# A hybrid attention trunk on one core: earlier loads for a triangular solve, loads in program order, and copies moved between engines

## Chip, core and metric

The kernel runs on one core of a Trainium2 chip. The metric is device time in microseconds (us): three runs of the kernel before took 3787.65, 3792.02 and 3792.04 us, median 3792.02.

The core has five engines, each with its own queue of instructions, worked off strictly in order: TensorE (PE in the profile; PEld is its loading of stationary operands), VectorE (DVE), ScalarE (ACT), GpSimd (POOL) and SyncE (SP), which here issues nearly all transfers (DMAs). SPq is SyncE's queue of DMA issues. Engines wait for each other by semaphores.

## What is computed

The reference is one layer of a transformer-like trunk over 2048 latent tokens (16 tiles of 128) and 256 context tokens (2 tiles), model width 1024:

```python
def sandwich_block(x, mod, g_norm, mixer, w_gu, w_down):
    sh1, sc1, gt1, sh2, sc2, gt2 = mod
    h = rmsnorm(x, g_norm[0]) * (1.0 + sc1) + sh1
    m, extra = mixer(h)
    x = x + gt1 * rmsnorm(m, g_norm[1])
    h = rmsnorm(x, g_norm[2]) * (1.0 + sc2) + sh2
    gate, up = jnp.split(h @ w_gu, 2, axis=-1)
    f = (jax.nn.silu(gate) * up) @ w_down
    x = x + gt2 * rmsnorm(f, g_norm[3])
    return x, extra
```

The mixer projects h by one matrix `w_in` and feeds three groups of heads: A is softmax attention with normalised and rotated queries and keys, B is a gated DeltaNet in both directions with a short convolution (its chunks of 64 need the inverse of a unit lower triangular matrix, `triangular_solve`), C is neighbourhood attention. Their outputs are joined and multiplied by `w_out`.

## The kernel before

The stages follow each other on TensorE, all in fp32 that is split into a high and a low part (`hi`, `lo`), so that each product takes three matmuls (`mm3`).

- **Phase B** (`phase_b`, to about 308 us): the adaLN vectors, h for six blocks of three tiles (stored to DRAM as `h_d`), the projection for group B, and its convolution. `conv(b)` runs one block late; for the last block the taps are added as each projection ends, and `conv_out` takes SiLU of it (L340), transposes it on TensorE and copies it out on VectorE (L353) to `y_d` (L354).
- **Phase AC** (`phase_ac`, to about 824 us) has two sweeps over the 18 tiles of h. The first multiplies each tile by three slices of 384 columns of `w_in` (c_cols: q, k, v of group C), the second by two of 320 columns (a_cols: q, k, v of group A) and, for the last three tiles, the third slice left over. One unit is one tile by one slice: 24 matmuls. A slice of weights comes in four pieces (`load_w`: tile wraw, three buffers) that ACT rounds (L255) and DVE subtracts (L256). Tiles of h (hi, lo, three buffers each) are loaded by `h_next`, one ahead per finished tile. In the second sweep each unit's result is copied by ACT (zn, four buffers, L449), normalised by head (L451 to L458, with POOL's power at L91), rotated on DVE and POOL (L470 to L475) and stored (zo).
- **Background work** rides on these sweeps. `Background.run(us)` takes pieces of a generator, each with an estimated cost, as long as its credit lasts. `prep` makes the DeltaNet operands of all tiles (it begins with `gates`). `bg` is the solve: five batches of up to 128 systems, three for the recurrence's first half. Each batch loads its systems from DRAM (B at L828, A at L829, tiles sB and sA), builds a matrix in sW (L833), and works through 76 pairs of a product (L843, into stmp) and a sum (L844) on DVE, each needing the one before; it ends with a copy (L847, into the same buffer as sA) and stores (L850, L851). sA and sW have one buffer, so a batch's loads wait for the stores of the batch before. A batch costs 26.9 of credit by the code's estimates. The third batch must be finished before group A begins (`need_solves(0)`), then `k_dups(4)` makes the last keys (KA, L1022 and L1023).
- **Group A** (to about 1625 us) runs one more piece of the solve per unit of 128 queries (L1242), **group C** follows (to about 1980 us), then the **output stage** (`phase_out`, to about 2225 us). There the weights `w_out` are scaled and split once (L1638 ACT, L1639 DVE) and each tile is multiplied, normalised and transposed; `h2_store` scales the transposed tile on ACT on its way out of PSUM (L1672, eight copies of 128 by 128 per tile). The **FFN** takes the rest.

The order on each queue is made when the program is built. The framework gives each instruction a priority by its place in the program, simulates the engines with its own cost estimates, and whenever an engine is free lets it take the ready instruction of highest priority. `tc.high_priority(offset=n)` moves instructions up by n places. `InOrder` (L28) pins an instruction behind everything traced before it on its engine, as long as its `on` is set; `self.sp` and `self.pe` are such wrappers, plain `nc.sync` is not. A pool's memory is by default waited for as a whole when a new pool takes its place; with `reuse_waits="tile"` each new tile waits only for the old tiles under it.

The lines around which the change turns are these:

```python
            for n in range(3):
                with tc.high_priority(offset=2 * HP if n == 0 else 0):
                    w = self.load_w(1680 + 384 * n, 384, wp, f"s{n}", ww=384, q=nc.scalar if n < self.WQ else None)
                Wc.append((c_cols, n, w, range(NT if n < 2 else NT - HB)))
                h_next()
            self.sp.dma_start(cos, a["cos"])
```

## Time and profile before

| | |
|---|---|
| median of three runs | 3792.02 us (3787.65 to 3792.04) |
| the profiled execution | 3788.4 us |
| its span, first to last instruction | 3786.6 us, mean granted clock 0.981 |
| PE busy in the span | 3608.3 us (95%) |
| DVE, ACT, POOL busy | 63%, 45%, 16% |
| DMA | 501.14 MB, mean 132 GB/s |

A row of the stretches gives a stretch in us from the span's start, its length, then busy us and count of instructions for PE, PEld, DVE, ACT and POOL, the share of full clock that was granted to TensorE, the busy share of the DMA engines and GB/s. A row of waits reads: engine, tile and line that waited, what it waited for, us in total, times, longest. A row of a timeline has start, duration, engine, line, operation, tiles and count. L37 is the wrapper through which TensorE's and much of SyncE's work is issued, so there the tile tells what it is. Durations come from one profiled execution; ends of matmuls are modelled.

### The profile page before, as it was taken

The page shows a single profiled execution, that of the slowest core. Times are in us where ns is not written, and L with a number is a line of the kernel's source. Part 1 is how long each engine was busy: PE and PEld are TensorE (multiplying, and loading weights), DVE is VectorE, ACT ScalarE, POOL GpSimd, SP SyncE. Part 2 cuts the span into 40 slices and gives each one's busy share as a digit, 9 for nine tenths or more (in the row PEclk, how much of TensorE's full clock was granted, in tenths as well). Part 3 has the DMA queues.
Part 4 walks back from the last instruction along what each step waited for, and adds up shares of the span by engine and source line. Part 5 has one row for each costly group of instructions (what it writes and reads, how often), then busy time and mean ns, then how long its engine had stood idle before and what let it go on. Part 6 is the DMA issues. An engine that isn't in the chain of part 4 may idle for free.

```text
span 3786.6 us, 64734 instructions
## 1 busy us (share of the span) xinstructions
PE 3608.3 (95%) x24526; PEld 3161.6 (83%) x24526; DVE 2399.1 (63%) x5030; ACT 1719.6 (45%) x3533; POOL 587.8 (16%) x859
## 2 busy tenths in 40 slices
PE   8997999979999999989999989999999999999999
PEld 5887988966777777768887879999999999888887
DVE  4784477689755555558775667778778777422433
ACT  4223222226666666656775653334334333322321
POOL 0002321630000000000003411111111111000121
PEclk9998999989999999999999999999999999999999
DMA  7555877842111221155315653334334332634653
GB/s 267 205 205 181 255 223 220 210 116 53 48 51 53 53 53 51 48 138 164 100 51 174 214 174 100 100 98 126 98 102 123 98 102 87 199 110 129 202 181 128
DMA packets 647496, 501.14 MB, mean 132 GB/s; under 512 B 253505, under 2 KB 576944, under 8 KB 644624
## 3 DMA queue, kind: packets, MB, share of 16 engines
q1 hardware_dynamic: 644400, 493.40, 43.3%
q8 instruction: 193, 3.16, 0.4%
q10 hardware_dynamic: 2624, 3.55, 0.3%
q14 instruction: 119, 0.97, 0.1%
q0 software_dynamic: 160, 0.05, 0.0%
HBM read 348.14 MB, written 148.73 MB: 131 GB/s over the span
## 4 chain that ended last, share of the span: by engine, by line
PE 74%; DVE 13%; ACT 4%; POOL 3%; DMA 3%; issue 3%; SPq 0%; ACTq 0%; POOLq 0%; DVEq 0%
PE pd L37 15%; PE Y L37 10%; PE pso L37 9%; PE pt L37 7%; PE X L37 7%; PE Z L37 6%; PE po L37 6%; PE rx L37 3%; PE m L37 2%; PE Sa L37 2%; DVE stmp L843 2%; PE S L37 2%; PE Sb L37 2%; DVE mx L1220 2%; DVE sW L844 1%
## 5 line engine op out<-in xcount | busy, mean ns | idle before, releaser
L1034 ACT ACTIVATE PT<-pt 128x512 f32<-128x512 f32 (+1 forms) x600 | 332.3, 554 | 257.9 <-PE pt L37 251.2
L37 PE MATMUL Y<-hop,raw 128*128 128x384 f32 x1788 | 338.6, 338 | 7.0 <-DVE u L1877 3.7
L37 PEld LDWEIGHTS Y<-hop,raw 128*128 128x128 f32 x1788 | 315.5, 188 | 8.6 <-DVE u L1877 4.7
L37 PE MATMUL po<-PT,V 128*64 128x256 f32 (+1 forms) x3072 | 314.8, 342 | 2.2 <-ACT PT L1034 1.9
L37 PE MATMUL pso<-whi,hi 128*128 128x384 f32 (+2 forms) x864 | 289.1, 335 | 24.8 <-ACT whi L255 13.0
L37 PE MATMUL pt<-ident,P 128*128 128x128 f32 x1752 | 285.1, 280 | 15.5 <-ACT PT L1034 7.9
L37 PE MATMUL pso<-whi,lo 128*128 128x384 f32 (+2 forms) x864 | 282.9, 327 | 8.4 <-DMA lo<-hl 8.4
L37 PE MATMUL pso<-wlo,hi 128*128 128x384 f32 (+2 forms) x864 | 283.1, 328 | 0.7 <-DVE wlo L256 0.5
L37 PEld LDWEIGHTS pt<-ident,P 128*128 128x128 f32 x1752 | 200.3, 141 | 94.8 <-ACT PT L1034 35.8
L37 PEld LDWEIGHTS po<-PT,V 128*64 128x64 f32 x3072 | 181.5, 137 | 79.2 <-issue 33.8
L37 PE MATMUL X<-hop,raw 128*128 128x384 f32 x1176 | 224.8, 339 | 3.4 <-DVE raw L1742 3.4
L37 PE MATMUL Z<-hop,raw 128*128 128x384 f32 x1188 | 223.6, 336 | 0.0
L1742 DVE TENSOR_TENSOR raw<-S,raw 128x512 fp32r<-128x512 f32 x198 | 145.9, 738 | 113.1 <-ACT raw L1741 108.1
L37 PEld LDWEIGHTS X<-hop,raw 128*128 128x128 f32 x1176 | 209.4, 189 | 4.1 <-DVE raw L1742 4.1
L37 PEld LDWEIGHTS Z<-hop,raw 128*128 128x128 f32 x1188 | 208.7, 187 | 0.1
L1889 POOL TENSOR_TENSOR o<-sg,p 128x384 f32<-128x384 f32 x66 | 89.2, 1351 | 740.7 <-DVE p L1888 365.8
L1741 ACT ACTIVATE raw<-S 128x512 fp32r<-128x512 f32 x198 | 124.6, 630 | 174.6 <-PE X L37 66.6
L37 PEld LDWEIGHTS pso<-whi,hi 128*128 128x128 f32 x864 | 168.5, 195 | 29.4 <-ACT whi L255 14.5
L37 PE MATMUL pd<-wd,ao 128*128 128x512 f32 x756 | 185.5, 394 | 0.0
L37 PE MATMUL pd<-wd,hop 128*128 128x512 f32 x756 | 183.0, 392 | 0.0
L971 POOL TENSOR_TENSOR rSe<-rS,eh 64x128 f32<-64x128 f32 x144 | 54.9, 400 | 810.6 <-DVE rS L1003 779.9
L37 PEld LDWEIGHTS pso<-whi,lo 128*128 128x128 f32 x864 | 168.0, 194 | 11.7 <-DMA lo<-hl 10.1
(346 smaller groups left out, 8273.9 us busy)
## 6 DMA issues: line engine op xcount, KB each, us to landing
hr<-a SPq DMA_DIRECT2D x72, 704.0 KB, 4.5
wr<-in_w_gu_dram SPq DMA_DIRECT2D x66, 512.0 KB, 4.0
wr<-in_w_gu_dram SPq DMA_DIRECT2D x132, 256.0 KB, 3.1
a<-o SPq DMA_DIRECT2D x396, 64.0 KB, 1.6
wm<-in_w_mod_dram SPq DMA_DIRECT2D x48, 512.0 KB, 4.2
hi<-hh SPq DMA_DIRECT2D x36, 512.0 KB, 5.2
lo<-hl SPq DMA_DIRECT2D x36, 512.0 KB, 6.0
st<-ptk SPq DMA_DIRECT2D x18, 768.0 KB, 4.2
```

Source lines behind the costliest of these rows:

```text
L37: r = f(*x, **kw)
L843: v.tensor_tensor(tv, M[:n, c0:c1, c0:i], M[:n, c0:i, i].unsqueeze(1).to_broadcast([n, m, k]), ALU.mult)
L844: v.tensor_reduce(M[:n, c0:c1, i], tv, AX.X, ALU.add)
L971: nc.gpsimd.tensor_tensor(Se[hh[x], d], S[hh[x], d, :, hh[x]], e.unsqueeze(2).to_broadcast([64, 2, 64]), ALU.mult)
L1034: self.nc.scalar.activation(out, p, AF.Copy)
L1220: nc.vector.tensor_reduce(mx[:, i:i + 1], S[:, :hi_ - lo_], AX.X, ALU.max)
L1741: self.nc.scalar.activation(hi, raw, AF.Copy)
L1742: self.nc.vector.tensor_tensor(lo, raw, hi.bitcast(F32), ALU.subtract)
L1889: nc.gpsimd.tensor_tensor(o[:, 0], sg, p1, ALU.mult)
```

## The change

- The loads of `dt_bias` and `a_log` move from `gates` (in phase AC) to the second block of phase B, into tiles of their own. Those of cos, sin and the norm gains gq move from the start of the first sweep to after its tiles 8 and 10.
- At the start of the first sweep the loads of h and of weights are pinned in program order: h of tile 0, first weights, h of tiles 1 and 2, second and third weights. Pools hp2 and wp2 take the finer reuse waits.
- The last block's `conv_out` gets priority over everything around it.
- The solve: the loads of each batch's systems get top priority. In the second sweep its pieces are taken only up to tile 11, 1.15 instead of 0.8 of credit a unit, and at raised priority. In group A it is 1.1 instead of 2.0 a unit. By the code's credits the third batch then ends at tile 8 of the second sweep (before: tile 12), the fourth at unit 17 of group A (7), the fifth at unit 41 (21).
- The output weights are split by halves of 512 columns, one tile for each half.
- `h2_store` makes four of its eight copies per tile on DVE.
- A one-column tile of the output stage shares another's buffers (s2, rss).

```diff
@@ -61,7 +61,7 @@
     INAC, ST = False, False
-    SW, SA = (4.2, 1.8, 3.4), 0.8
+    SW, SA = (4.2, 1.8, 3.4), 1.15
@@ -305,6 +305,7 @@
             nc.sync.dma_start(self.mi, a["mi"])
+            self.dt, self.al = self.ctile("dt", [128, 8]), self.ctile("al", [128, 8])
@@ -385,9 +386,13 @@
                     conv(b - 1)
+                if b == 1:
+                    nc.sync.dma_start(self.dt, a["dt_bias"].rearrange("o d h -> o (d h)").to_broadcast([128, 8]))
+                    nc.sync.dma_start(self.al, a["a_log"].rearrange("o d h -> o (d h)").to_broadcast([128, 8]))
                     self.mod_part(1 if b == 1 else 2, sb, xp, psm)
-            conv_out(NB - 1, yl)
+            with tc.high_priority(offset=3000):
+                conv_out(NB - 1, yl)
@@ -402,8 +407,8 @@
             cst = es.enter_context(tc.tile_pool(name="pin_c", bufs=1))
-            hp = es.enter_context(tc.tile_pool(name="hp2", bufs=HB))
-            wp = es.enter_context(tc.tile_pool(name="wp2", bufs=1))
+            hp = es.enter_context(tc.tile_pool(name="hp2", bufs=HB, reuse_waits="tile"))
+            wp = es.enter_context(tc.tile_pool(name="wp2", bufs=1, reuse_waits="tile"))
@@ -547,7 +552,11 @@
                                 prep.run(us)
-                                self.bg.run(us2 if prep.left else us3)
+                                if w == 0:
+                                    self.bg.run(us2 if prep.left else us3)
+                                elif t0 < 12:
+                                    with tc.high_priority(offset=HP):
+                                        self.bg.run(us3)
@@ -555,18 +564,29 @@
             Wc = []
+            self.sp.on = True
             for n in range(3):
+                if n < 2:
+                    h_next()
                 with tc.high_priority(offset=2 * HP if n == 0 else 0):
-                    w = self.load_w(1680 + 384 * n, 384, wp, f"s{n}", ww=384, q=nc.scalar if n < self.WQ else None)
+                    w = self.load_w(1680 + 384 * n, 384, wp, f"s{n}", ww=384)
                 Wc.append((c_cols, n, w, range(NT if n < 2 else NT - HB)))
-                h_next()
-            self.sp.dma_start(cos, a["cos"])
-            self.sp.dma_start(sin, a["sin"])
-            gsrc = a["g_qk_a"]
-            self.sp.dma_start(gq[:, 0:6, :], gsrc[0, 0:1, :].unsqueeze(1).to_broadcast([128, 6, 64]))
-            self.sp.dma_start(gq[:, 6:8, :], gsrc[0, 1:2, :].unsqueeze(1).to_broadcast([128, 2, 64]))
-            nc.vector.tensor_scalar(gq[:, 0:6, :], gq[:, 0:6, :], 0.125, None, ALU.mult)
-            sweep(0, Wc, *self.SW)
+                if n == 0:
+                    h_next()
+            self.sp.on = self.INAC
+
+            def rotary(t):
+
+                if t == 8:
+                    self.sp.dma_start(cos, a["cos"])
+                    self.sp.dma_start(sin, a["sin"])
+                if t == 10:
+                    gsrc = a["g_qk_a"]
+                    self.sp.dma_start(gq[:, 0:6, :], gsrc[0, 0:1, :].unsqueeze(1).to_broadcast([128, 6, 64]))
+                    self.sp.dma_start(gq[:, 6:8, :], gsrc[0, 1:2, :].unsqueeze(1).to_broadcast([128, 2, 64]))
+                    nc.vector.tensor_scalar(gq[:, 0:6, :], gq[:, 0:6, :], 0.125, None, ALU.mult)
+
+            sweep(0, Wc, *self.SW, rotary)
@@ -650,10 +670,7 @@
         nc.scalar.activation(self.beta, self.ba[:, :, 0:8], AF.Sigmoid)
-        dt = wk.tile([128, 8], F32, name="dt")
-        al = wk.tile([128, 8], F32, name="al")
-        self.sp.dma_start(dt, a["dt_bias"].rearrange("o d h -> o (d h)").to_broadcast([128, 8]))
-        self.sp.dma_start(al, a["a_log"].rearrange("o d h -> o (d h)").to_broadcast([128, 8]))
+        dt, al = self.dt, self.al
@@ -825,8 +842,9 @@
                 r0 = 128 * e + 64 * bi if bi < 2 else 16 * e
-                nc.sync.dma_start(B[q], self.bt_d[bi // 2][r0:r0 + ns, fs])
-                nc.sync.dma_start(A[q], self.low_d[e][bi].rearrange("s (j i) -> s j i", j=64)[:, fs, fs])
+                with self.tc.high_priority(offset=3000):
+                    nc.sync.dma_start(B[q], self.bt_d[bi // 2][r0:r0 + ns, fs])
+                    nc.sync.dma_start(A[q], self.low_d[e][bi].rearrange("s (j i) -> s j i", j=64)[:, fs, fs])
@@ -1239,7 +1257,7 @@
                             nc.vector.reciprocal(rs[:, qi, h2:h2 + 1], sm[:, 3:4] if n > 1 else sm[:, 0:1])
-                            self.bg.run(2.0)
+                            self.bg.run(1.1)
@@ -1600,7 +1618,7 @@
                 self.mm3(mt[t][:, s], [hi[:, k] for k in range(KD)], [lo[:, k] for k in range(KD)],
-                         [WH[k][:, s] for k in range(KD)], [WL[k][:, s] for k in range(KD)])
+                         [WH[n][:, k] for k in range(KD)], [WL[n][:, k] for k in range(KD)])
@@ -1611,7 +1629,7 @@
                 sq = wk.tile([128, 1024], BF16, tag="rjunk", name="sq2", bufs=1)
-                s2 = wk.tile([128, 1], F32, tag="s2", name="s2")
+                s2 = wk.tile([128, 1], F32, tag="rss", name="s2")
@@ -1627,16 +1645,18 @@
             v.tensor_copy(ym[:, 5:8], self.goc)
-            WH, WL = [], []
+            WH, WL = [[cst.tile([128, KD, 512], F32R, name=f"W{x}{n}") for x in "HL"] for n in range(2)]
+            WH, WL = [WH[0], WL[0]], [WH[1], WL[1]]
                 raw = self.wraw[k]
-                WH.append(cst.tile([128, 1024], F32R, name=f"WH{k}"))
-                WL.append(cst.tile([128, 1024], F32R, name=f"WL{k}"))
-                nc.scalar.activation(WH[k], raw, AF.Copy, scale=ym[:, k:k + 1])
-                v.scalar_tensor_tensor(WL[k], raw, ym[:, k:k + 1], WH[k].bitcast(F32), ALU.mult, ALU.subtract)
+                for n in range(2):
+                    r = raw[:, 512 * n:512 * n + 512]
+                    nc.scalar.activation(WH[n][:, k], r, AF.Copy, scale=ym[:, k:k + 1])
+                    v.scalar_tensor_tensor(WL[n][:, k], r, ym[:, k:k + 1], WH[n][:, k].bitcast(F32), ALU.mult,
+                                           ALU.subtract)
@@ -1669,8 +1689,12 @@
                 k = 4 * g + j
-                self.nc.scalar.activation(h2[:, k], p[:, 128 * j:128 * j + 128], AF.Identity,
-                                          bias=self.b2[:, vv, k:k + 1], scale=self.s2[:, vv, k:k + 1])
+                if g:
+                    self.nc.vector.tensor_scalar(h2[:, k], p[:, 128 * j:128 * j + 128], self.s2[:, vv, k:k + 1],
+                                                 self.b2[:, vv, k:k + 1], ALU.mult, ALU.add)
+                else:
+                    self.nc.scalar.activation(h2[:, k], p[:, 128 * j:128 * j + 128], AF.Identity,
+                                              bias=self.b2[:, vv, k:k + 1], scale=self.s2[:, vv, k:k + 1])
```

## Prediction

> **What bounds the kernel now.** The first part of the page was read first, then busy time by stretch, then the waits of TensorE in the worst stretches, then the queue that issues DMAs (SPq) behind those waits.
>
> ```profile
> span 3786.6 us, 64734 instructions
> PE 3608.3 (95%) x24526; PEld 3161.6 (83%) x24526; DVE 2399.1 (63%) x5030; ACT 1719.6 (45%) x3533; POOL 587.8 (16%) x859
> ```
>
> TensorE is busy for 95% of the span, and the change takes no matmul away. So it can win only from the 178 us in which PE stands idle, and from the time in which it runs at half clock. The stretches say where that is (columns: stretch, length, busy time and count of PE, PEld, DVE, ACT, POOL, granted clock, DMA share, GB/s).
>
> ```profile
> 307.00:365.00 58.00, 35.99 (x157) 30.42 (x156) 21.64 (x52) 18.16 (x36) 13.25 (x42) 0.71 0.75 233
> 500.00:600.00 100.00, 87.87 (x557) 79.74 (x556) 78.21 (x225) 25.62 (x47) 31.71 (x33) 0.93 0.72 218
> 650.00:660.00 10.00, 7.86 (x41) 7.20 (x41) 9.64 (x32) 3.51 (x12) 0.32 (x2) 0.83 0.42 121
> 662.00:742.00 80.00, 73.95 (x497) 72.67 (x496) 47.62 (x130) 20.47 (x57) 55.72 (x104) 0.99 0.81 208
> 752.00:822.00 70.00, 51.62 (x313) 50.12 (x311) 58.65 (x218) 11.89 (x32) 29.02 (x49) 0.90 0.38 101
> 822.00:850.00 28.00, 18.23 (x80) 13.63 (x80) 20.68 (x66) 13.67 (x28) 3.50 (x12) 0.76 0.67 162
> 850.00:1000.00 150.00, 142.47 (x1302) 105.52 (x1300) 136.00 (x440) 102.44 (x215) 8.00 (x20) 1.00 0.24 60
> 1000.00:1150.00 150.00, 148.24 (x1454) 113.35 (x1454) 83.60 (x181) 103.34 (x212) 9.09 (x24) 1.00 0.18 50
> 2220.00:2260.00 40.00, 25.16 (x133) 23.39 (x132) 28.99 (x35) 25.98 (x49) 2.55 (x5) 0.87 0.67 207
> ```
>
> Three places matter: the seam into the first sweep (307 to 365, 22.0 us idle), the end of the second sweep with the start of group A (752 to 850, 28.2 us idle), and the seam into the FFN (2220 to 2260, 14.8 us idle). The half clock costs besides: at 0.71 over 58 us, 16.8 us of clock are missing, so PE was granted half speed for 33.6 us; the long waits below lie in 16.6 us of that, and the other 17 us of half-speed work lose 8.5 us. Hence the first seam costs 30.5 us.
>
> **Seam into the first sweep: small loads moved, loads in program order, last convolution first.** TensorE's waits between 300 and 365 (us in total, times, longest), then the queue SPq by time (start, us), and one row of the chain that ended last:
>
> ```profile
> PE pso L37 <- ACT whi L255: 13.0, 2, 11.5
> PE pso L37 <- DMA lo<-hl: 5.1, 1, 5.1
> PE pst L37 <- DVE es L353: 3.1, 2, 1.8
> ```
>
> ```profile
> 324.74 1.03 SPq L354 DMA_DIRECT2D y<-es  x1
> ...
> 338.09 0.65 SPq L37 DMA_DIRECT2D gq<-in_g_qk_a_dram  x1
> ...
> 339.81 8.00 SPq L37 DMA_DIRECT2D al<-in_a_log_dram  x1
> 347.86 1.91 SPq L37 DMA_DIRECT2D wraw<-in_w_in_dram  x2
> ```
>
> ```profile
> 314.64 7.97 DMA lo<-hl
> ```
>
> The 11.5 us wait is for the second weight slice. Its last two wraw pieces are issued at 347.86, right behind the load of a_log, which held the queue for 8.00 us behind the many small rows of gq. After the change dt and al are loaded in phase B, cos and sin at tile 8 and gq at tile 10 of the sweep. The queue may stand for the same 8.00 us there; three tiles of h are held then, three units of 24 matmuls each per tile, so I cost that at nothing. If that cover were gone it would cost those 8 us again.
>
> The new order on SPq is h of tile 0, first weights, h of tiles 1 and 2, second and third weights, pinned behind everything traced earlier on that queue: the last store of y. That store (now at 324.7 and later) needs the last SiLU on ACT; beside it two rows of the DMA issues, whose last column is the median time to landing:
>
> ```profile
> 301.71 2.13 ACT L340 ACTIVATE yl<-yl 128x2304 f32<-128x2304 f32 x1 [2.40 <-DVE yl L328]
> ```
>
> ```profile
> hi<-hh SPq DMA_DIRECT2D x36, 512.0 KB, 5.2
> lo<-hl SPq DMA_DIRECT2D x36, 512.0 KB, 6.0
> ```
>
> The SiLU ends at 303.8; with its transposes and six copies put first I estimate the store, and the pinned loads behind it, at 310.4. Landing takes 6.0 us, so the sweep starts at 316.4, where it now stalls until lo has landed, 314.64 + 7.97 = 322.6. Left are 6 us idle and some 6.8 us at half speed (3.4 us lost), 9.4 in all: the gain is 30.5 - 9.4 = 21 us. Bounds: 8 (only the 8.00 us of the queue go) and 27 (all but the 3.4). I take 21, since the 13.0 us wait has no other cause left. Finer reuse waits of the two pools add nothing: the pinned loads come later than the last reader of the old tiles. One wait is new: the fourth piece of the first weights needs one of three wraw buffers, and h of tiles 1 and 2 is queued behind it on SPq. They are wanted one and two units after the start (3.6 us each by the row of 662 to 742); a landing of 6.0 us against that leaves up to 3 us, within the lower bound.
>
> **Second sweep: the third batch of the solve.** TensorE's waits from 735 to 860, SPq by time, and groups of instructions (busy us, mean ns, idle before), the last two of PE from 660 to 740:
>
> ```profile
> PE pt L37 <- DVE KA L1023: 10.2, 1, 10.2
> PE pso L37 <- DMA hi<-hh: 8.6, 2, 6.9
> PE pt L37 <- DVE q L1028: 3.7, 1, 3.7
> ```
>
> ```profile
> 661.29 0.62 SPq L851 DMA_DIRECT2D sysN<-sW  x1
> ...
> 706.74 0.61 SPq L829 DMA_DIRECT2D sA<-low  x1
> ...
> 743.03 0.61 SPq L829 DMA_DIRECT2D sA<-low  x1
> ```
>
> ```profile
> L843 DVE TENSOR_TENSOR stmp<-sW 128x112 f32<-128x112 f32 (+31 forms) x380 | 113.2, 329 | 1.3
> L844 DVE TENSOR_REDUCE sW<-stmp 128x8 f32<-128x112 f32 (+31 forms) x380 | 81.2, 243 | 1.2
> ```
>
> ```profile
> L37 PE MATMUL pt<-ident,qd 128*128 128x128 f32 x11 | 1.8, 299 | 3.7 <-DVE q L1028 3.7
> L37 PE MATMUL pt<-ident,kd 128*128 128x128 f32 x12 | 1.6, 272 | 0.0
> ```
>
> The second batch is stored at 661.3, but the third one's loads go out at 706.7 and 743.0, behind other traffic of the queue; so its arithmetic fell on 752 to 822, and the last keys (KA) waited 10.2 us behind it. One batch is 380/5 = 76 pairs of 329 + 243 ns, 43 us of DVE. At top priority the loads go at about 662.
>
> What does DVE have free? Between 662 and 742 no solve ran: 497 matmuls less some 11 + 12 transposes are 474/24 = 20 units in 80 us; a unit takes PE 3.6 us and DVE 47.62/20 = 2.4 us. With 43 us over the some 20 units that are left before tile 12, DVE needs 4.5 us a unit, 0.9 more than PE: a backlog of 18 us, of which the z buffers (4) and the banks (3) take about 4 units, 14 us. The last 12 units carry no solve and give 1.2 us each back. By the credits in the code (0.13 + 0.00208 mk a pair, 1.15 a call) the third batch ends at tile 8, and a third of the fourth (14 us of DVE) is queued by tile 12 as well; this backlog PE does feel.
>
> Now lost from 735 to 850: 3.7 + 18.4 + 9.8 us idle; the missing clock is 70 x 0.10 + 28 x 0.24 = 13.7 us, about half of it on idle: 7. That is 39. Afterwards: 4 from the third batch, 14 from the fourth, 4 of half clock and 2 at the start of group A, 24. Gain 15 us; bounds 5 (the backlog keeps the stores of zo, and h behind them, as late as now) and 30 (the fourth batch finds its loads too late to be in the way).
>
> The half clock is a term of its own: in 650 to 660 PE idles 2.1 us in all, and yet the granted clock is 0.83, 3.4 us at half speed. The Trainium skill (TensorE: Matmul & The Clock Gate, Part 1 on the clock gate) says that the clock drops after at least one idle window of about 3.4 us. By this rule the short waits left in the second sweep would cost no clock, and the sum would be 4 us better; the row disagrees, and I keep the term.
>
> **Group A** gets 1.1 instead of 2.0 of solve per unit. PE idles 7.5 us in 850 to 1000 and 1.8 in the next 150, where no solve runs: the crowding costs 5.7. Spread thinner I take 2.5; bounds 0 and 5.
>
> **Output weights by halves, norms' copies.** TensorE's waits from 1975 to 2260, the group that moves, and the nearest row for its new engine (min/median/max ns):
>
> ```profile
> PE X L37 <- ACT p L1841: 10.5, 1, 10.5
> PE m L37 <- DVE WL L1639: 4.5, 5, 2.4
> PE m L37 <- DVE lo L1591: 3.6, 4, 1.5
> PE Y L37 <- ACT raw L1741: 3.1, 1, 3.1
> ```
>
> ```profile
> L1672 ACT ACTIVATE raw<-pst,b,s 128x128 f32<-128x128 f32 x144 | 52.2, 473 | 1.8 <-PE pst L37 1.8
> ```
>
> ```profile
> L709 DVE TENSOR_SCALAR sbs<-pb x2: 279/279/279, 379.3 to 382.9; 128x128 f32<-128x128 f32 x1, 16x128 f32<-16x128 f32 x1
> ```
>
> Halves let the first product start half a piece earlier, for 8 more instructions on ACT and 8 more on DVE: of the 4.5 us I take 1 (bounds -1 and 3). Of the 144 copies 72 move: ACT is relieved of 72 x 52.2/144 = 26 us, DVE gets 72 x 0.279 = 20 us (nearest row: the same shape out of PSUM), both beside PE's work. Only two tiles at the FFN seam lie on the path: 4 x 0.363 = 1.45 us less on ACT ahead of p and of raw each, against 4 x 0.279 = 1.1 us more on DVE ahead of the sums. I take 1.5 (bounds -2 and 6), and -1 for the waits on lo (0 to -2), since DVE's queue gets longer in each tile.
>
> The first batches of the solve (500 to 600, 12.1 us idle) keep their work and place: 0, bounds -6 and 5, as their loads move too.
>
> Sum: 21 + 15 + 2.5 + 1 + 1.5 - 1 + 0 = 40 us. The profiled execution took 3788.4 us (1.8 around its span) and the median of the three runs is 3792.0; 3788.4 - 40 = 3748.4, and on the median's footing 3752. All lower bounds together give 3, all upper ones 76.
>
> **Rivals.** (1) *Only the first seam shrinks*: the backlog of DVE eats the second sweep's gain. For it: in 752 to 822 DVE is busy for 84% and PE loses 18.4 us beside one batch; against it: the tail without solves. 40 - 15 = 25, 3767 us. A rule here speaks against the change as well: the Trainium skill (SBUF — State Buffer, SBUF: two separate sides) says that a VectorE instruction with two SBUF inputs and a GpSimd instruction lock each other out for its whole length, and the solve's products meet GpSimd's rotary parts. By that rule this rival would hold, with its 3767 us.
>
> ```profile
> L470 POOL TENSOR_TENSOR zu<-zn,sin 128x160 f32<-128x160 f32 x11 | 5.9, 540 | 7.3 <-DVE zn L458 7.1
> L470 POOL TENSOR_TENSOR zu<-zn,sin 128x160 f32<-128x160 f32 x4 | 3.4, 852 | 4.7 <-DVE zn L458 3.5 <-DVE stmp L843 1.2
> ```
>
> Without the solve (670 to 745) this instruction took 540 ns, beside it 852: 0.3 us a unit, 6 us over 20 units, on an engine with room; so it costs the path little here, and the trace agrees with the rule only in part.
> (2) *Only the second sweep shrinks*: the loads pinned behind the last y store start late and the weights come as late as now; 40 - 21 = 19, 3773 us. For it: one late store now holds every load. Against: 8.00 us of queue time vanish whatever the order.
> (3) *All goes*: the scheduler finds room for everything, 66 us, 3726.
> (4) *Slower*: in the second sweep the 57 us of solve at raised priority stand ahead of each tile's norms, and PE waits for all of it. Each idle us costs a quarter more in clock (7 on 28): 71; the stores of zo come late and with them h, 10 us as in 752 to 822; 81 in place of 39, 42 lost against 25 gained elsewhere: 3809 us. It decides once PE loses over 72 us from the sweep's start to group A.
>
> **How the numbers follow.** Forecast 0.50, rival 1 0.20, rival 2 0.12, rival 3 0.10, rival 4 0.08. The likeliest case gives 3752. The range 3727 to 3783 goes up past rivals 1 and 2 with some of their spread, and down to rival 3; above it is rival 4, and a little of the rest on both sides. About 0.2%, 7.6 us, is what a measurement of this kernel can tell from no change. The forecast, rival 3 and three quarters of rivals 1 and 2 lie beyond that: faster 0.84; the rest of those two is 0.08; slower 0.08.
>
> **What would show it.** Right: no load of a_log or gq between 300 and 365, the wait of pso on whi under 3 us, full clock before 335; loads of sA within 5 us of the second batch's stores; the wait on KA under 3 us; DVE over 90% busy in the first two thirds of the second sweep; the wait of X on p between 9 and 11 us. Wrong: the first matmul of the sweep after 320; new waits on h or zn in the second sweep of over 25 us; the loads of sA still behind the stores of zo; idle time in 500 to 600 over 18 us.

## The result, and the profile after

The changed kernel takes 3828.33 us (median of 5 runs, 3824.54 to 3829.94) against 3792.02 us before, run beside it: a ratio of 1.0097, 95% interval 1.0082 to 1.0112. It is 36 us slower; the prediction said 40 us faster. The profiled execution took 3828.3 us (before 3788.4). The first part of its page:

```profile
span 3826.5 us, 64732 instructions
...
PE 3605.3 (94%) x24526; PEld 3159.4 (83%) x24526; DVE 2432.4 (64%) x5110; ACT 1699.0 (44%) x3471; POOL 588.1 (15%) x859
```

TensorE's work is what it was (3605 us against 3608); its idle time grew from 178 to 221 us. Busy time by stretch (columns as in the prediction):

```profile
307.00:365.00 58.00, 37.37 (x191) 32.37 (x190) 24.41 (x54) 20.18 (x41) 16.26 (x46) 0.82 0.77 236
...
500.00:600.00 100.00, 86.35 (x569) 77.15 (x568) 72.98 (x189) 27.43 (x52) 30.57 (x32) 0.97 0.76 229
650.00:660.00 10.00, 8.35 (x46) 8.35 (x47) 7.35 (x24) 2.55 (x8) 4.39 (x9) 0.83 0.61 140
...
1000.00:1150.00 150.00, 147.84 (x1447) 113.16 (x1447) 85.87 (x186) 102.19 (x212) 9.07 (x24) 1.00 0.22 57
```

The first seam is a little better, the steady stretches are what they were. To find the place of the loss, the same matmul was looked up in both traces, stage by stage. It stands later in the changed kernel by: +0.6 us at the end of phase B; -3.4 once the first sweep runs; -4.2 at the start of the second sweep; **+58.4 at the first score of group A**; +48.7 at the end of group A; +51.5 at the end of group C; +43.1 at the end of the output stage; +39.9 at the end. So all of the loss, 62.6 us, is made in the second sweep, and the other stages together give some 23 us back. TensorE's waits from 595 to 885 us (us in total, times, longest):

```profile
PE pso L37 <- ACT zn L454: 32.7, 5, 14.0
PE pso L37 <- DMA lo<-hl: 17.1, 3, 12.0
PE pt L37 <- DVE q L1046: 13.9, 2, 12.0
PE pt L37 <- DVE KA L1041: 9.4, 1, 9.4
PE pso L37 <- DMA hi<-hh: 6.7, 2, 3.4
```

The wait on KA is there still (10.2 before, 9.4 now). New are the 32.7 us for zn, of which there were 2.7 before. The first line is from the kernel before, the second is ScalarE's own wait in the changed one, over the stretch that is defined below:

```profile
PE pso L37 <- ACT zn L449: 2.7, 2, 2.1
```

```profile
ACT zn L454 <- DVE zo L477: 32.6, 4, 16.8
```

A bank of products cannot be filled since ScalarE has not copied the earlier one out, and it has not because no buffer of zn is free. The buffers come free when VectorE and GpSimd are through with a tile's norm and rotation.

**What VectorE does in that time.** One stretch is used from here on: from the start of the second sweep's third unit to the first score of group A, 647.8 to 827.1 us before, 643.6 to 885.6 after. First before, by the stretch's busy times (VectorE's is the third after the length), then VectorE's own waits in it:

```profile
647.80:827.10 179.30, 148.32 (x942) 144.15 (x941) 129.55 (x413) 40.74 (x112) 94.81 (x176) 0.93 0.62 162
```

```profile
DVE zn L456 <- POOL qr3r L91: 23.2, 16, 2.2
DVE zn L456 <- POOL qr5r L91: 21.5, 15, 2.3
```

And the same two views after:

```profile
643.60:885.60 242.00, 156.22 (x943) 151.72 (x941) 196.40 (x709) 40.39 (x110) 102.39 (x180) 0.83 0.56 139
```

```profile
DVE zn L461 <- POOL qr5r L91: 21.5, 17, 2.4
DVE zn L461 <- POOL qr3r L91: 17.3, 17, 1.4
```

VectorE sums a tile's squares, GpSimd makes the factor of the norm from the sum (lines 89 and 91), VectorE scales with it. VectorE works its queue in order, so while it stands at that scaling everything behind it stands too. Before, it was busy for 129.6 us and stood for 44.7: 174.3 of 179.3 us. After, 196.4 and 38.8: 235.2 of 242.0. **VectorE was full in both kernels**, though its busy share was 72% before. The stretch grew by 62.7 us, VectorE's busy time by 66.9, its stands by -5.9. What grew is the solve (groups of VectorE in the stretch, before, then after; busy us, mean ns):

```profile
L843 DVE TENSOR_TENSOR stmp<-sW 128x96 f32<-128x96 f32 (+22 forms) x92 | 28.8, 344 | 0.2
L844 DVE TENSOR_REDUCE sW<-stmp 128x4 f32<-128x16 f32 (+19 forms) x93 | 20.7, 251 | 0.2
```

```profile
L861 DVE TENSOR_TENSOR stmp<-sW 128x224 f32<-128x224 f32 (+36 forms) x238 | 71.9, 333 | 0.9
L862 DVE TENSOR_REDUCE sW<-stmp 128x4 f32<-128x16 f32 (+23 forms) x239 | 51.6, 244 | 0.9
```

93 pairs fell into the stretch before, 238 of the 380 after: the third and the fourth batch are done before group A begins, and the fifth but for its last 6 pairs. (Instructions overlap at their ends; counted once, the pairs take 45 us before and 110 after, and with the first and last steps of each batch 49 and 120. The expectations below use 45 and 115.)

**The first seam.** The queue SPq by time (start, us), and one of its waits between 300 and 350:

```profile
308.44 0.33 SPq L37 DMA_DIRECT2D cos<-in_cos_dram  x1
...
309.29 1.02 SPq L37 DMA_DIRECT2D gq<-in_g_qk_a_dram  x2
...
312.83 2.18 SPq L355 DMA_DIRECT2D y<-es  x3
315.06 0.63 SPq L37 DMA_DIRECT2D hi<-hh  x1
321.50 1.22 SPq L37 DMA_DIRECT2D lo<-hl  x1
322.76 4.13 SPq L37 DMA_DIRECT2D wraw<-in_w_in_dram  x3
```

```profile
SPq L37 <- DMA gq<-in_g_qk_a_dram: 5.8, 1, 5.8
```

The program asks for cos and sin at tile 8 and for gq at tile 10, but inside the raised priority of the sweep's hook and with nothing to wait for; in the queue they stand ahead of the last stores of y. gq took 12.0 us to land, and lo of the first tile waited 5.8 us for it. The first weights (wraw) went out behind lo, and when ScalarE had rounded them the sweep began, at 331.0 us and not at the 316.4 of the prediction. TensorE's 22.0 us of waiting became one of 17.1 us for those weights and some small ones.

### The profile page after: what moved, and what is told of

It reads as the page before. It is cut to its first block, busy times and chain, and to the rows that moved or that the text cites. A ratio compares the mean times of both kernels' runs of the same rounds, so it can differ in the third digit from the quotient of the medians.

```text
span 3826.5 us, 64732 instructions
## 1 busy us (share of the span) xinstructions
PE 3605.3 (94%) x24526; PEld 3159.4 (83%) x24526; DVE 2432.4 (64%) x5110; ACT 1699.0 (44%) x3471; POOL 588.1 (15%) x859
## 3 DMA queue, kind: packets, MB, share of 16 engines
q1 hardware_dynamic: 644400, 493.40, 43.1%
## 4 chain that ended last, share of the span: by engine, by line
PE 77%; DVE 11%; ACT 4%; POOL 3%; DMA 3%; issue 3%; SPq 1%; ACTq 0%; DVEq 0%; POOLq 0%
PE pd L37 15%; PE Y L37 10%; PE pso L37 8%; PE pt L37 7%; PE X L37 7%; PE Z L37 7%; PE po L37 6%; PE m L37 4%; PE rx L37 4%; DVE stmp L861 2%; PE Sa L37 2%; PE Sb L37 2%; PE S L37 2%; DVE sW L862 1%; ACT P L1246 1%
## 5 line engine op out<-in xcount | busy, mean ns | idle before, releaser
L37 PE MATMUL pso<-whi,hi 128*128 128x384 f32 (+2 forms) x864 | 289.5, 335 | 57.8 <-ACT zn L454 32.7
L37 PE MATMUL pt<-ident,P 128*128 128x128 f32 x1752 | 284.2, 280 | 10.6 <-ACT PT L1052 4.5
L1766 DVE TENSOR_TENSOR raw<-S,raw 128x512 fp32r<-128x512 f32 x198 | 146.8, 742 | 107.0 <-ACT raw L1765 102.0
```

The costliest lines, as they stand in the source:

```text
L37: r = f(*x, **kw)
L1766: self.nc.vector.tensor_tensor(lo, raw, hi.bitcast(F32), ALU.subtract)
```

## The experiments

Theories of the loss. **A**: the pieces of the solve at raised priority stand ahead of the norms in VectorE's queue. **B**: the loads at top priority hold SPq ahead of h. **C**: the loss comes from other edits. As the runs came in, a fourth was formed, here **the account**: VectorE is full in the second sweep, by work and by standing for GpSimd, so whatever brings more of the solve into it lengthens it by as much. Times are medians, each with its ratio to the kernel before on the same chip (whose medians there were 3786 to 3788 us).

**The solve as before, all else changed (e1).** In the changed kernel:

```diff
-    SW, SA = (4.2, 1.8, 3.4), 1.15
+    SW, SA = (4.2, 1.8, 3.4), 0.8
-  if w == 0:
-      self.bg.run(us2 if prep.left else us3)
-  elif t0 < 12:
-      with tc.high_priority(offset=HP):
-          self.bg.run(us3)
+  self.bg.run(us2 if prep.left else us3)
-  with self.tc.high_priority(offset=3000):
       nc.sync.dma_start(B[q], self.bt_d[bi // 2][r0:r0 + ns, fs])
-  self.bg.run(1.1)
+  self.bg.run(2.0)
```

> The changed kernel with all four edits of the solve taken back (loads at normal priority, pieces at normal priority in all tiles of the second sweep, 0.8 us a unit, 2.0 in group A); the seam, the output weights and the norms' copies stay changed. Theory A (the raised pieces stand ahead of the norms in VectorE's order): the second sweep's loss of some 60 us goes and group A's gain of 10 goes with it, so 3828 - 50 = 3778 us, and the waits of pso on zn in the second sweep fall from 32.7 us to under 5. Theory B (the loads at top priority hold the queue SPq ahead of h): the same total, as these are taken back too; e2 and e3 part the two. Theory C (the loss in the second sweep comes from other edits, for example the other start of the first sweep): the time stays within 10 us of 3828.

3772.07 us, 0.9959 (0.9947 to 0.9972). The stretch is 178.7 us and the wait on zn 3.0. C falls: the four edits of the solve cost 56 us of time, and the rest of the change is a gain of 0.4%.

**The pieces unraised (e2); the loads unraised (e3).** Each of the two priorities alone taken back in the changed kernel:

> The changed kernel with one edit taken back: the pieces of the solve in the second sweep run at normal priority; they are still dropped from tile 12 on, still get 1.15 us a unit, and the loads of the systems stay at top priority. Theory A: most of the loss goes, the waits of pso on zn (32.7 us) fall under 8 and the time is 3785 +- 10 us; the 12.0 us wait on lo stays. Theory B: the loads set where the batches run, so the time stays above 3815 us.

> The changed kernel with one edit taken back: the loads of the systems (sA, sB) at normal priority; the pieces keep their raised priority. Theory A: only the 12.0 us wait on lo at 664 us goes, where SPq stood 5.8 us at a load of sB that waits for VectorE's first step of the third batch, so 3810 to 3818 us, with over 25 us of pso waiting for zn left. Theory B: the second sweep's loss goes, under 3785 us.

3798.73 us, 1.0030 (1.0019 to 1.0042), and 3794.23 us, 1.0014 (1.0005 to 1.0023). Neither A nor B alone: taking back the one recovers 30 us, the other 34, and with the other edit still in place 27 and 22 us are lost against the 3772 us of e1. The waits on zn miss A's forecasts too: 25.5 us in the first (A: under 8) and 10.5 in the second (A: over 25). The stretch has 168 pairs of the solve in the first and 141 in the second.

**Each edit alone, on the kernel before:** only the loads at top priority (e6), and later only the raised pieces (1.15 us, up to tile 11; e16):

> The kernel before with one edit alone: the loads of the systems at top priority. The prediction has the third batch then start at about 662 us and the last keys wait no longer: at 0.8 us a unit a gain of 10 to 15 us, 3778. Theory Q (any early third batch stands between the steps of the norms, at normal priority too): the waits of pso on zn in the second sweep rise by 15 us or more, and the time is 3795 to 3815 us. In both, the loads of sA go out within 5 us of the second batch's stores.

> The kernel before with the raised pieces alone: 1.15 us a unit at raised priority up to tile 11 of the second sweep, none after; the loads at normal priority, group A at 2.0. Theory P: the third batch's loads still go out late, some 705 to 745 us, so the batch falls beside the last tiles as before and costs 0 to 10 us more: 3786 to 3798 us. Theory Q: 3805 us or more, with waits on zn of over 20 us.

The loads alone: 3818.32 us, 1.0074 (1.0060 to 1.0088), 32 us slower with not one piece raised. The pieces alone: 3807.01 us, 1.0053 (1.0040 to 1.0067). The first is the edit from which the prediction had most of its gain in the second sweep; its time lies 3 us above the range of theory Q, and the wait for the last keys, which was to go, grew from 10.2 to 17.0 us. Its stretch, and VectorE's waits in it:

```profile
643.00:856.80 213.80, 154.87 (x943) 150.34 (x941) 163.60 (x566) 40.88 (x110) 101.61 (x180) 0.87 0.57 145
```

```profile
DVE zn L456 <- POOL qr5r L91: 22.1, 16, 2.3
DVE zn L456 <- POOL qr3r L91: 14.9, 14, 3.3
```

163.6 us of work, 37.0 of standing, 13.2 of other idle time: again VectorE is what fills the stretch. With the pieces alone the loss comes late: up to 796 us the kernel is 3.0 us behind the kernel before, at the first score 25.6 (its trace is of a run of 3798.9 us). TensorE's longest wait there is one of 15.4 us for VectorE in the middle of the solve; those on zn are 10.6, so theory Q has the time right and not the place.

**Twice the buffers of zn (e9)** in the changed kernel (`bufs=4` to `bufs=8`):

> The changed kernel with 8 buffers in place of 4 for zn, the copy of a tile's q or k that TensorE's next bank waits for. Theory Q (a norm takes long because pieces of the solve stand between its steps, so the buffers come late): twice the buffers hold twice the norms under way, the waits of pso on zn fall from 32.7 to under 10 us, and the time to 3800 to 3812 us. Theory V (VectorE is simply behind, and the wait moves to whatever comes last): the waits on zn go but those on q and KA grow by about as much, 3820 to 3830 us.

3828.84 us, 1.0112 (1.0098 to 1.0126): nothing. The waits on zn fell to 23.4 us (theory Q: under 10) and those on KA, kd and Sa grew. More buffers did not help here, where VectorE is full, so the wait on zn was a sign and not the cause.

**Four buffers of sB (e8)**, for theory B. SPq in the changed kernel:

```profile
656.16 1.80 SPq L847 DMA_DIRECT2D sA<-low  x2
658.06 2.85 SPq L37 DMA_DIRECT2D hi<-hh  x2
660.95 1.14 SPq L37 DMA_DIRECT2D kd<-in_cache_a_k_dram  x1
667.95 1.72 SPq L846 DMA_DIRECT2D sB<-bt  x4
669.77 0.53 SPq L37 DMA_DIRECT2D hi<-hh  x1
670.34 3.53 SPq L37 DMA_DIRECT2D lo<-hl  x3
```

The four loads of sB at 667.95 are those of the fifth batch, two batches early: they had to wait until the third had read its buffer, at 667.9, and lo, behind them, came for a matmul that waited 12.0 us.

> The changed kernel with 4 buffers in place of 2 for sB, so that no load of sB at top priority has to wait for VectorE's first step of an earlier batch. In the changed kernel SPq stood 5.8 us at such a load from 662 us on, with lo of the next tile behind it, and TensorE then waited 12.0 us for lo. Theory B (that place costs what it shows): the wait on lo at 664 us goes, 12 us and some 4 us of half clock, 3810 to 3816 us. Theory V (VectorE is what is behind, so a tile that starts earlier waits longer for its zn): the wait on lo goes, the waits on zn grow, 3822 to 3830 us.

3817.05 us, 1.0084 (1.0071 to 1.0098): 11 us better, and the wait of 12.0 us on lo is 3.3. B is right for this one place, within 1 us of its range. The trace says more: the stretch has 205 pairs in place of 238, so part of the gain is less solve in it.

**No GpSimd in the norm (e5).** In the changed kernel, the two instructions that make the factor on VectorE (the root is left out):

```diff
-  r = self.rstd(wa, ss, n, 1.0 / 64, f"qr{n}")
+  nc.vector.tensor_scalar(r, ss, 1.0 / 64, EPS, ALU.mult, ALU.add)
+  nc.vector.reciprocal(r, r)
```

> The changed kernel, with the two GpSimd instructions between the sum of squares and the scaling of q and k (sum to mean, then to the power -0.5) replaced by two VectorE instructions (mean, then reciprocal): the square root of these norms is left out. In the changed kernel, between 640 and 885 us, VectorE stands 38.8 us in 34 places until GpSimd has made that factor, 1.14 us each, with everything behind it in its order. Theory P (these stalls are what made a tile cost VectorE more than its busy time says): the stalls go, the second sweep's loss of 60 us falls by over 25, so under 3803 us. Theory Q (what counts is how many pieces of the solve stand between two steps of one norm): the gain is under 12 us, the waits of pso on zn stay over 20 us.

3797.27 us, 1.0029 (1.0019 to 1.0039): 31 us come back, as theory P had it. But the waits on zn stay at 25.9 us: VectorE has 191.3 us of work in 209.7 and is still full.

**The same without leaving anything out:** ScalarE takes the root, VectorE the reciprocal (the lines that set up the tiles r and eps are not shown). First on the kernel with the solve as before and the small loads pinned (e13; that kernel is e7, below), then alone on the kernel before (e18), last on the whole changed kernel with four buffers of sB (e15):

```diff
-  r = self.rstd(wa, ss, n, 1.0 / 64, f"qr{n}")
+  nc.scalar.activation(r, ss, AF.Sqrt, bias=eps, scale=1.0 / 64)
+  nc.vector.reciprocal(r, r)
```

> The kernel of 3769 us with the factor of the q and k norms made by ScalarE (square root) and VectorE (reciprocal) in place of GpSimd's two instructions; nothing is left out. In the second sweep of this kernel VectorE stands 44.6 us in 31 places until GpSimd has made that factor. Theory P (in-order stalls are part of what a tile costs VectorE): they fall under 15 us, the third batch ends earlier and the wait on KA (9.1 us) with it: 3758 to 3764 us. Rival: VectorE has slack here, ScalarE's table has to be loaded and its queue gets longer: 3768 to 3774 us.

> The kernel before with the norm factor by ScalarE and VectorE and nothing else changed. Account: 129 us of busy time and 45 us of stands make 97% of the 179 us of the stretch, so without the stands TensorE becomes the limit: the stretch is about 160 us, as in the kernel of 3754 us, and the time 3766 to 3772 us against 3786. Rival (VectorE has room as its busy share says, 129 of 179 us): within 4 us of 3786.

> The whole changed kernel with 4 buffers of sB and the norm factor by ScalarE and VectorE. Theory P: 3828 less 11 (the buffers, measured) less the stalls; at 34 stalls of 1.14 us with a quarter more in clock some 40 to 48, so 3770 to 3780 us. Theory Q: raised pieces in front of the norms cost as much as before, 3795 us or more.

3754.33 us, 0.9915 (0.9902 to 0.9929), the fastest kernel of this study; 3766.45 us, 0.9946 (0.9931 to 0.9960); 3804.78 us, 1.0050 (1.0037 to 1.0063). The stretch of the second one, with its ScalarE groups, and the stretch of the third:

```profile
647.00:806.40 159.40, 144.59 (x943) 142.17 (x941) 135.36 (x449) 51.06 (x149) 48.85 (x104) 0.95 0.70 181
```

```profile
L457 ACT ACTIVATE qr5r<-qss,eps 128x5 f32<-128x5 f32 x18 | 5.4, 300 | 34.0 <-DVE qss L455 34.0
L457 ACT ACTIVATE qr3r<-qss,eps 128x3 f32<-128x3 f32 x18 | 5.3, 297 | 36.4 <-DVE qss L455 36.4
```

```profile
646.40:858.20 211.80, 155.52 (x943) 151.96 (x941) 199.61 (x749) 50.60 (x147) 56.85 (x108) 0.86 0.63 159
```

In the kernel before, this one small edit wins 21 us: the stretch is 159.4 us, VectorE idles 24 of them, and TensorE is busy for 91%. In the changed kernel with four buffers of sB the same edit wins 12 us only (from 3817): VectorE works for 199.6 of 211.8 us, so there the solve itself is too much. Theory P, that the stands are the whole reason, falls with this run (it said 3770 to 3780).

**The raised loads on norms without the stands (e14)**, that is e13 with them and four buffers of sB:

> The kernel of 3754 us (norm factor by ScalarE and VectorE, solve as before) with the loads of the systems at top priority and 4 buffers of sB. On the norms with GpSimd's factor, these loads alone cost 32 us. Theory P (the stalls are the reason): without them VectorE has the room that the prediction gave it, 4.5 us a unit against 3.6 of TensorE with the z buffers between, so the early third batch costs nothing: 3745 to 3758 us, waits of pso on zn under 10 us. Theory Q (a batch beside the tiles costs time whatever the norms wait for, as its pieces stand between their steps): 3764 to 3785 us, waits on zn over 15 us.

3767.64 us, 0.9950 (0.9938 to 0.9963): 13 us slower than without them, where they cost 32 us beside the stands. Theory P is missed by 10 us; the time is in theory Q's range, though the waits on zn (8.6 us) are under the 15 that Q asked for. How the 32 us divide is not shown, since less of the solve falls into the stretch as well: 29 pairs more than in e13, against 75 more in e6. Nor is the solve free without the stands: 9.8 us more of VectorE's work made the stretch 14.6 us longer (174.4), though VectorE idles for 29.4 us of it. It is full in places, those where the third batch meets the norms:

```profile
700.00:730.00 30.00, 22.83 (x147) 22.32 (x146) 29.90 (x126) 8.76 (x26) 9.73 (x19) 0.94 0.65 170
```

There VectorE works for 29.9 of 30 us and TensorE for 22.8. So the account, drawn up over the whole stretch, holds for the kernels with GpSimd's factor; without it VectorE has to be read piece by piece.

**The third batch's loads alone (e17)** at top priority on the kernel before, the run by which the account could fail:

> The kernel before with the loads of the third batch alone at top priority (the fourth's and fifth's stay as they were). From the start of the second sweep to the first score of group A the traces so far add up as VectorE's busy time, its stands for GpSimd and 5 to 13 us of other idle time; the solve in it was 45 us before (179 us long), 83 with all loads raised (214), 115 in the changed kernel (242). Account: with the fourth batch held back the solve in the stretch stays at 45 to 60 us, and the stretch at 179 to 195 us: 3786 to 3803 us, no gain from the early third batch. The prediction's view (the third batch out of the way of the last keys frees them): the stretch shortens by 10 to 15 us, 3772 to 3778 us.

3796.04 us, 1.0025 (1.0015 to 1.0035). Its stretch, and TensorE's waits from 595 to 885:

```profile
650.40:841.60 191.20, 151.69 (x941) 147.85 (x941) 144.12 (x491) 40.26 (x109) 99.86 (x180) 0.90 0.65 168
```

```profile
PE pso L37 <- ACT zn L449: 22.4, 6, 8.3
PE Sa L37 <- DVE KA L1024: 6.2, 1, 6.2
...
PE pt L37 <- DVE KA L1024: 2.9, 1, 2.9
```

The waits for the last keys fall less than the prediction said of the early third batch: they are 2.9 and 6.2 us in place of 10.2 and 1.9, and zn comes on top with 22.4. The account (179 to 195 us) holds. This run also prices one early batch: the same matmul stands 2.6 us later than in the kernel before at 670 us, ahead of the third batch (684 to 763), and 29.7 later at 742. The sixty microseconds without solve behind it give nothing back until 792; then 12 us come back, where the kernel before has its own third batch. The stretches together:

| kernel | pairs of the solve | length us | VectorE busy | stands for GpSimd | rest |
|---|---|---|---|---|---|
| before | 93 | 179.3 | 129.6 | 44.7 | 5.0 |
| third loads alone | 132 | 191.2 | 144.1 | 42.5 | 4.6 |
| pieces alone | 141 | 204.3 | 146.8 | 48.7 | 8.8 |
| all loads alone | 168 | 213.8 | 163.6 | 37.0 | 13.2 |
| changed, four sB | 205 | 224.4 | 179.3 | 35.4 | 9.7 |
| changed | 238 | 242.0 | 196.4 | 38.8 | 6.8 |
| changed, four sB, root on ScalarE | 241 | 211.8 | 199.6 | 0 | 12.2 |
| before, root on ScalarE | 93 | 159.4 | 135.4 | 0 | 24.0 |
| e13 (solve as before, root on ScalarE) | 93 | 159.8 | 135.3 | 0 | 24.5 |
| e14 (e13, loads raised, four sB) | 122 | 174.4 | 145.1 | 0 | 29.4 |

Busy time, stands and rest make up the length by their nature. What the table shows is that the rest is small wherever GpSimd makes the factor.

**The first seam.** The small loads pinned at tiles 8 and 10, in the changed kernel (e4), and then in the kernel with the solve as before (e7):

```diff
   def rotary(t):
+      self.sp.on = t in (8, 10)
       if t == 8:
...
+      self.sp.on = False
```

> The changed kernel with the loads of cos, sin and gq pinned where the program has them, at tiles 8 and 10 of the first sweep; in the changed kernel they ran at 308 to 310 us, before the last stores of y, and SPq then stood 5.8 us until gq had landed, ahead of lo of the first tile. Theory S1 (gq's load is what made the sweep start at 331 and not at 316): the sweep starts 5 to 8 us earlier, at 323 to 326 us, and the time at the end of the seam falls by as much, with some 2 us of clock besides. Theory S2 (the pinned order behind the stores of y alone sets it): the start stays within 2 us of 331. The second sweep is not touched by this edit; its total is compared up to 650 us only.

> The changed kernel with the solve's four edits taken back (as in the run of 3772 us) and the loads of cos, sin and gq pinned at tiles 8 and 10. Theory S1 (the first seam's time is worth what it is at the seam): the start of the sweep at 324 us in place of 331, and the whole 10 us are kept, 3762 us. Theory S3 (the first sweep's end is set by the chain that prepares and solves the systems, and time won at the seam is waited away between 505 and 600): 3769 to 3773 us, with 5 us or more of added idle time of TensorE between 500 and 600.

3827.95 us, 1.0105 (1.0091 to 1.0118), and 3769.21 us, 0.9955 (0.9942 to 0.9967): neither time differs from that of its kernel without the edit by what can be measured. Yet the sweep starts at 323.7 us in the first (331.0 without), and TensorE is 9.8 us further at the end of the seam. S1 is right at the seam. By 600 us nothing is left of it in the first kernel, as S3 had it. The changed kernel with the loads pinned, from 500 to 520, and TensorE's waits from 505 to 600:

```profile
500.00:520.00 20.00, 13.97 (x84) 12.69 (x83) 20.00 (x71) 3.57 (x7) 3.12 (x3) 0.83 0.73 221
```

```profile
PE pg L37 <- DVE pL L816: 7.2, 2, 5.8
PE ptr L37 <- issue: 6.8, 2, 5.2
PE ptr L37 <- DVE py L759: 3.4, 2, 2.1
```

VectorE is busy for 20.00 of 20 us there, with the first batch of the solve; TensorE, come earlier, waits for it. With the solve as before (e7) the kernel is 16.0 us ahead of the kernel before at 360 us, and 8.6 at the end of the first sweep; without the pinned loads (e1) it was 5.1 and 2.4. So part of the gain stays there by the traces, 6 of 11 us, though the two times do not show it.

**Group A's rate, the norms' copies, the halves**, each on the kernel of 3769 us: 1.1 put in (e10); all copies on ScalarE again (e11); weights in whole pieces again (e12).

```diff
-  self.bg.run(2.0)
+  self.bg.run(1.1)
```

```diff
-  if g:
-      self.nc.vector.tensor_scalar(h2[:, k], p[:, 128 * j:128 * j + 128], self.s2[:, vv, k:k + 1],
-                                   self.b2[:, vv, k:k + 1], ALU.mult, ALU.add)
-  else:
   self.nc.scalar.activation(h2[:, k], p[:, 128 * j:128 * j + 128], AF.Identity,
                             bias=self.b2[:, vv, k:k + 1], scale=self.s2[:, vv, k:k + 1])
```

```diff
-  for n in range(2):
-      r = raw[:, 512 * n:512 * n + 512]
-      nc.scalar.activation(WH[n][:, k], r, AF.Copy, scale=ym[:, k:k + 1])
+  nc.scalar.activation(WH[k], raw, AF.Copy, scale=ym[:, k:k + 1])
```

> The kernel of 3769 us (changed seam, output and norms' copies; the solve as before; small loads at tiles 8 and 10) with one edit of the solve put in again: 1.1 us in place of 2.0 a unit in group A. The prediction's term: 2.5 us of gain (0 to 5), 3767 us. Rival: the gain of 10 us that group A showed in the changed kernel came from the rate, 3759 us; the other rival: it came from the solve being done earlier, so the rate alone changes nothing or, as the batches end later than group A wants them, costs time: 3769 us or more.

> The kernel of 3769 us with all the norms' copies on ScalarE again (the output weights stay in halves). By the prediction's terms (+1.5 at the FFN seam, -1 for the waits on lo) this costs 0.5 us, 3770 us. Rival: the 6 to 8 us that the output stage gained come from these copies, since they stand on ScalarE between the tiles: 3775 to 3778 us, and the wait of Y on raw is 3.1 us again in place of 1.7.

> The kernel of 3769 us with the output weights in whole pieces of 1024 columns again (the norms' copies stay split). By the prediction's term the halves are worth 1 us (-1 to 3): 3770 us. Rival, from the run with all copies on ScalarE, whose output stage still gained 3.7 us: the halves are worth that, 3772 to 3774 us, and waits of m on WL of 2 us and more come back.

3767.35 us, 0.9952 (0.9940 to 0.9965); 3775.38 us, 0.9973 (0.9963 to 0.9983); 3771.80 us, 0.9962 (0.9950 to 0.9975). With the rate group A gains 2.5 us on the kernel before by the traces, the prediction's own figure, but 0.6 of them are there without it; group C loses 3.5. The copies are worth 6 us by the times, whose intervals just meet (the trace of e11 is of a run of 3781.7 us). The halves are worth 2 to 3: the times cannot tell, but the first products of the output stage gain 1.0 us on the kernel before with whole weights and 3.9 with halves. Groups of the copies in the changed kernel, and two waits of TensorE at the FFN seam with all copies on ScalarE:

```profile
L1696 ACT ACTIVATE raw<-pst,b,s 128x128 f32<-128x128 f32 x72 | 27.0, 460 | 0.3 <-PE pst L37 0.3
...
L1693 DVE TENSOR_SCALAR raw<-pst,s,b 128x128 f32<-128x128 f32 x72 | 24.6, 404 | 29.9 <-PE pst L37 29.8
```

```profile
PE X L37 <- ACT p L1858: 10.5, 1, 10.5
...
PE Y L37 <- ACT raw L1758: 3.1, 1, 3.1
```

With the copies split these two are 9.6 and 1.7 us.

## Why the prediction was wrong

**The step that failed** is in "What does DVE have free?" It took 47.62 us of busy time over 20 units, "DVE 47.62/20 = 2.4 us" a unit beside TensorE's 3.6, and so a room of 32 us in those 80. VectorE's waits in the very same 662 to 742 us of the kernel before:

```profile
DVE zn L456 <- POOL qr3r L91: 15.8, 9, 2.2
DVE zn L456 <- POOL qr5r L91: 14.9, 9, 2.3
```

47.6 and 30.7 us are 78.3 of 80: there was no room. Where the sum has "4 from the third batch", the run with its loads alone (e17) lost 27 us while that batch ran. What looked like idle time was the head of the queue standing, and pieces of the solve fill it only where the queue has them between the sum of squares and the scaling; the stands went from 44.7 to 38.8 us while the solve grew by 70. Hence the backlog is not 18 us, "of which the z buffers (4) and the banks (3) take" 14, but all that is added.

**A second step was too small**: by the credits, a third of the fourth batch, 14 us, was to fall before group A. It was the whole fourth and all but 6 pairs of the fifth. The credits say where the program asks for a piece; where it runs is set by priority and by when its data are there. With the loads raised and no credit changed, 168 pairs ran in the stretch in place of 93.

Term by term:

- *Second sweep, +15 (5 to 30)*: -62.6. The sA loads did go out 2.5 us after the second batch's stores (653.65 to 656.16), but the waits for the last keys fell by 3 us only when the third batch alone came early (e17), and grew when all loads did (e6).
- *Rival 4 (slower, 3809 us, chance 0.08)* had the sign, and in part the mechanism: the raised pieces alone cost 21 us. The loads alone, with every piece at normal priority, cost 32, so it named the lesser half. Its rule "once PE loses over 72 us" was right: TensorE lost 85.8 us in the stretch.
- *Rival 1* ("the backlog of DVE eats the second sweep's gain") was the right question, answered "against it: the tail without solves"; there was no such tail, since the fourth and fifth batch ran in it, and in e17, which has one from 763 to 823 us, it gave nothing back before 792. The rule that it leaned on (the Trainium skill, SBUF — State Buffer, SBUF: two separate sides: VectorE with two inputs and GpSimd lock each other out) would show in longer instructions. The traces agree with it on both engines: GpSimd's rotary part, 540 ns without the solve, took 690 in the changed kernel from 713 to 860, and VectorE's instructions with two inputs that met one of GpSimd's were longer than the same shapes alone, by 14.2 us in all in the stretch before and 14.1 after. Most of that is the rotation (zo, 11.5 and 10.3 us); the solve's products went from 1.0 to 3.2, and reductions, with one input, were no longer. So the lock-out is there, and it is not what grew.

```profile
L475 POOL TENSOR_TENSOR zu<-zn,sin 128x160 f32<-128x160 f32 x14 | 9.7, 690 | 14.3 <-DVE zn L463 6.0 <-DVE zo L479 5.7 <-DVE stmp L861 2.3
```

- *First seam, +21 (8 to 27)*: 3.4, below the bounds. The mechanism held in part (no load of a_log there any more), but "cos and sin at tile 8 and gq at tile 10 of the sweep" did not happen, and the last y store went at 312.8 to 315.0, not 310.4. Pinned where the program has them, the start is 323.7: 9.8 us of the missing time were gq's. The rest of the late start, 7.3 us, is the last store (4.7) and the first weights, which the sum left out: their loads stand behind lo, and with ScalarE's rounding they were ready 8.6 us after the first load of h, not 6.0 (2.6).
- *500 to 600, 0 (-6 to 5)*: right for the change (idle 13.6 us against 12.1). But it is where a gain of the seam ends: of the 13 us that the changed kernel with pinned small loads (e4) was ahead of the kernel before, 10 went there.
- *Half clock as a term of the second sweep*: the granted clock fell from 0.93 to 0.83 in the stretch; by the account this has no price of its own, since TensorE waits for VectorE at either speed (no run tries it). The single short spell is there again (650 to 660: clock 0.83). TensorE idles for only 1.65 us in that row, but it had stood for 4.0 us on zn from 647.7 to 651.7, so here the trace agrees with the rule of the Trainium skill (TensorE: Matmul & The Clock Gate, Part 1) that was weighed against the term, one idle window of about 3.4 us. Against the rule speaks the kernel before alone, with one wait of 2.1 us ahead of its spell.
- *Group A, +2.5*: 9.7 in the change, since no solve is left in it after 900 us; the rate alone gives 1.9 (2.5 less the 0.6 that are there without it).
- *Output weights +1, copies +1.5, lo -1*: 8.4 us in the output stage and its seam, 1.2 more at the FFN's. Runs of each: 2 to 3 for the halves, 6 for the copies. VectorE's copy took 404 ns, not the 279 of the row taken for it, and still paid. The likely reason is that TensorE waited for ScalarE's queue (p and raw above); this is argued and not shown.
- *X on p, 9 to 11 us*: 9.6. Between the FFN's first tiles and its last product of Z another 5 us are won, and 3 lost after that. Such a gain, 2 to 6 us, is there in the other kernels with the copies split, and 0.9 or none in those without; how the copies reach so far, and where the 3 go, is not settled.
- *The signs*: of the four signs of being wrong two came, the first matmul of the sweep after 320 us (331.0) and new waits on zn of over 25 us (32.7). Of the sum, one figure is off: all lower bounds together give 2 us, not 3.

## What to carry to other kernels

An engine's room is its time less its busy time *less the time in which the head of its queue stands*; read its own waits before work is given to it, and where they add up to the stretch, it is the bound, whatever its busy share says. Read this where the added work will run, not over the whole stretch. Work that is put earlier by a priority brings along all that had been held back by the same late load, so the question is how much of it falls before the next point at which others wait. And before looking for a better place for background work, shorten the round trip that makes the engine stand: one small edit there was worth 21 us here, more than all the moves.

## What the runs showed of the hardware

- A factor of 3 to 5 numbers a partition made by GpSimd cost VectorE's queue 44.7 us in 31 places before, 1.44 us each; ScalarE's root took 0.30 us, and with it VectorE stood 4.0 us for the factor in the whole stretch.
- gq, two broadcast loads of small rows (192 KB the larger), took 12.0 us to land, where 512 KB of h took 4.9 in the median, and lo, behind it on the queue, waited 5.8 us for that. The load of hi ahead of lo took 12.5 us, against 5.2 with gq moved away (e4).
- A load that waits for its buffer holds all loads behind it on SPq: 5.8 us at one load of sB became 12.0 us of waiting for lo on TensorE, and 3.3 with two more buffers (e8).
- VectorE's instructions with two inputs were longer where they met one of GpSimd's, by 14 us in all in the stretch, in either kernel; reductions were not.
